# Cleared matrix images in DRAM for the base inverses of a gated DeltaNet, and a last token tile in two column halves

## The chip, the cores and the metric

The kernel runs on one core of a Trainium2 chip. The metric is device time in microseconds (us) of one execution; where several runs are given, it is their median. The engines are named as in the profile: PE is TensorE (PEld its weight loads), DVE is VectorE, ACT is ScalarE, POOL is GpSimd, and SP is SyncE, whose queue issues nearly all DMA transfers of this kernel. L549 means line 549 of the kernel's file.

## The reference

One layer of a bidirectional hybrid encoder: 1024 tokens of width 1024, all in float32. Three sub-layers follow one another, each with an RMS norm before and after it and a residual sum:

- a mixer that is half windowed attention and half a bidirectional gated DeltaNet (4 heads, key and value width 128, chunks of 64 tokens, two directions), with one projection in and one out
- cross attention into 256 memory tokens
- a SwiGLU network of width 2816

The part that the change touches most is the triangular solve of the DeltaNet. For each head, direction and chunk:

```python
tmat = lower + jnp.eye(c, dtype=jnp.float32)
rhs = jnp.concatenate([v * beta[..., None], kb * jnp.exp(g)[..., None]], axis=-1)
sol = lax.linalg.triangular_solve(tmat, rhs, left_side=True, lower=True, unit_diagonal=True)
```

The other part is the end of the layer, `x = x + _rms_norm(f, g_ffn_post)`, where `f` is the product with `w_down`. The norm of a token needs the sum of squares over all 1024 columns of `f`.

## The kernel before, in words

Every product in full precision is made of three matmuls on float32r parts (`split`, L99 to L106: ACT makes the high part, L103, and DVE or POOL the low part, L104). A tile scheduler fixes the order of instructions on each engine when the program is built, from a list of steps written by hand (`ORDER_1`, `ORDER_2`, `ORDER_3`, L37 to L39) and from priorities. Within an engine the order then stands. SP's queue is in order too: a transfer whose wait is not over holds back all that stand behind it, and in the program's own list a transfer also waits for the transfer eight places before it to have landed.

**ORDER_1** (about 20 to 220 us of the profiled execution). Projections of q, k and v with a short convolution (`conv`, L287 on DVE), the decays (E), the turned keys (K), key products (U), query products (C), and `base_inverse` (B, L522 to L556) for each of two groups `g` of two heads. It takes the 32x32 diagonal blocks of the strictly triangular key products, 128 of them side by side (64 in each direction), one per partition, and inverts them by 30 elimination steps on DVE (L545, L547). Two scaled results remain: `V`, the transposed inverses, and `A`, the plain ones, both as 128 partitions of 32x32. Four DMAs (L554) put them into the DRAM tensors `d_inv`, 4 KB a partition.

**ORDER_2** (about 220 to 360 us). Projections for the attention (A, V), the gate (G), the first attention windows (W) and four `levels` (L, L558 to L632), one per head, which build the 128x128 inverses of both directions from the 32x32 ones in two steps (32 to 64, 64 to 128):

- `fetch` (L564) reads four block columns from `d_inv` (`cz` and `cw`, each for two directions, 128 partitions of 8 x 32 numbers, in pieces of 128 bytes). POOL copies strips of them into `m5`, `c5` and `c6` (L575 to L578).
- Each of two parts (4 chunks each) widens `c5`, `c6`, `cz0` and `cz1` into 128x128 matrices with zeros off the diagonal blocks: `D5`, `D6`, `Z0` and `Z1`, by a product with the mask `dmask` on DVE (L588, 128x512 numbers an instruction).
- The part loads `Ul` (key products, L591), transposes it on PE (L595), masks it into `L5` and `L6` on DVE (L596, L597), and makes two pairs of products (L604 and L610): `L5` with `m5`, then `D5` with the result, which fills the second diagonal into `D6`, `Z` and `mov6` (L615 to L624); then `L6` with `mov6`, and `D6` with the result, which fills the last quarter of `Z` (L626, L627). L629 stores both `Z` into `d_pz`.

`D5`, `D6`, `Z0`, `Z1` have two buffers each, so a level's `Z` tiles wait for the stores of the level before. PE takes up matmuls of the projections (L262) between the steps of a level, in the fixed order.

**ORDER_3** (about 360 to 560 us). The scan over chunks, which loads `kv` and `pz` from DRAM, beside the other windows and the memory's keys and values. Then follow the output projection, cross attention and SwiGLU.

**The end.** The last product (L1773 to L1786) takes four token tiles `t`, each of 33 matmuls of 512 columns into one PSUM bank `X[t]`. Behind each tile (L1787 to L1797): add to `zv` (L1791, DVE), sum of squares (`sq_of`, L1706, ACT), gain (L1793, DVE), root by `rstd_at` (L1721 and L1722, POOL), two sums with the residual (L1796, DVE) for the halves `za` and `zv`, and two output writes (L1797). For the last tile nothing is left that this could lie beside.

## Time and profile before

| what | value |
|---|---|
| median of 3 runs | 1525.34 us (1525.03 to 1528.78) |
| the profiled execution, its own time | 1531.03 us |
| its span in the trace | 1529.3 us, 1.7 us less |
| granted PE clock, mean | 0.994 of full |
| DMA moved | 261.06 MB in 275159 packets |

The profile is one execution of 1531.03 us. Stretches and durations are read from it; a difference that is worked out in it is then set against the median. The stage of the levels is found in it by L588 (first at 220.0, last at 340.0 us) and by the stores of L629 (256.3 to 361.7 us). The views used below are: the page; a table of stages (busy time of each engine in a stretch); groups of instructions by line; waits (who waited for whom); the timeline (single instructions); the DMA view; and the chain of work that ended last.

### The profile page before, as it was taken

How to read it: one execution, taken by the hardware profiler on the slowest of the kernel's cores; microseconds unless marked ns; L12 is line 12 of the kernel's file. 1: busy time of each engine (PE TensorE's matmuls, PEld its weight loads, DVE VectorE, ACT ScalarE, POOL GpSimd, SP SyncE). 2: the span in 40 equal slices, each digit the busy share in tenths (PEclk: the TensorE clock that was granted, in tenths of full speed). 3: DMA queues.
4: the chain of work that ended last, by engine and by line, in shares of the span. 5: the costliest groups of instructions: out<-in, count | busy, mean ns of one | idle time of the engine just before them, and what ended most of it. 6: DMA issues, size and time to landing. Idle time of an engine off the chain costs nothing.

```text
span 1529.3 us, 21202 instructions
## 1 busy us (share of the span) xinstructions
PE 1475.7 (96%) x7403; PEld 1239.1 (81%) x7403; DVE 1116.3 (73%) x1805; ACT 752.0 (49%) x1541; POOL 364.1 (24%) x369
## 2 busy tenths in 40 slices
PE   6999999998999999999999999999999999999997
PEld 5888888877889778888788877888888888888786
DVE  6868999787888866538567768676867774696665
ACT  5578821447557764455544685223222332454532
POOL 2020221311226203252201002433534342000021
PEclk9999999999999999999999999999999999999999
DMA  6235575856987584458725554343434333853355
GB/s 208 76 109 148 144 194 142 218 176 173 322 279 236 186 296 152 141 167 271 241 97 173 192 182 134 97 138 116 146 109 153 124 103 111 321 208 97 104 177 167
DMA packets 275159, 261.06 MB, mean 171 GB/s; under 512 B 34904, under 2 KB 206829, under 8 KB 275053
## 3 DMA queue, kind: packets, MB, share of 16 engines
q1 hardware_dynamic: 275053, 259.71, 53.9%
q8 instruction: 58, 0.95, 0.3%
q14 instruction: 48, 0.39, 0.1%
HBM read 181.25 MB, written 75.79 MB: 168 GB/s over the span
## 4 chain that ended last, share of the span: by engine, by line
PE 61%; DVE 10%; DMA 10%; ACT 4%; issue 3%; SPq 2%; POOL 1%; DVEq 0%; POOLq 0%; ACTq 0%
PE pD L1481 7%; PE pE L1481 7%; PE pA L1481 6%; PE pmg L1071 6%; PE pdX L1687 6%; PE pst L1287 5%; PE pcq L262 4%; PE pB L1481 3%; PE psc L810 2%; PE pdA L1687 2%; PE pdD L1687 2%; PE pg L262 2%; DMA wraw<-in_w_gate_up_dram 1%; PE pco L1186 1%; PE pdX L1784 1%
## 5 line engine op out<-in xcount | busy, mean ns | idle before, releaser
L103 ACT CAST whi<-wraw 128x1024 fp32r<-128x1024 f32 x96 | 100.8, 1051 | 133.0 <-DMA wraw<-in_w_gate_up_dram 37.0
L262 PE MATMUL pg<-hlo,whi 128*128 128x512 f32 x352 | 139.1, 396 | 0.0
L262 PE MATMUL pg<-hhi,whi 128*128 128x512 f32 x352 | 139.1, 396 | 0.0
L262 PE MATMUL pg<-hhi,wlo 128*128 128x512 f32 x352 | 138.1, 393 | 0.0
L104 POOL TENSOR_TENSOR wlo<-wraw,whi 128x1024 fp32r<-128x1024 f32 x36 | 88.3, 2453 | 189.6 <-ACT whi L103 188.2
L1481 PE MATMUL pA<-b,whi 128*128 128x512 f32 x352 | 111.9, 400 | 3.6 <-ACT m L1508 2.8
L104 DVE TENSOR_TENSOR wlo<-wraw,whi 128x1024 fp32r<-128x1024 f32 x60 | 76.0, 1269 | 46.0 <-ACT whi L103 42.4
L1481 PEld LDWEIGHTS pA<-b,whi 128*128 128x128 f32 x352 | 66.5, 192 | 19.2 <-ACT m L1508 4.0
L1687 PE MATMUL pdX<-dhl,whi 128*128 128x512 f32 x264 | 76.1, 390 | 1.5 <-ACT dhl L103 0.8
L262 PEld LDWEIGHTS pg<-hhi,whi 128*128 128x128 f32 x352 | 66.3, 189 | 13.4 <-ACT hhi L103 0.2
L262 PEld LDWEIGHTS pg<-hhi,wlo 128*128 128x128 f32 x352 | 66.2, 188 | 12.8
L262 PEld LDWEIGHTS pg<-hlo,whi 128*128 128x128 f32 x352 | 66.2, 188 | 12.7
L1564 POOL TENSOR_TENSOR act<-act,up 128x512 f32<-128x512 f32 x33 | 50.7, 1538 | 83.1 <-DVE up L1563 61.8
L1481 PE MATMUL pA<-b,wlo 128*128 128x512 f32 x176 | 69.9, 398 | 0.5 <-DVE wlo L104 0.5
L103 ACT CAST whi<-araw 128x1024 fp32r<-128x1024 f32 (+1 forms) x36 | 35.3, 982 | 67.9 <-PE pdX L1687 27.6
L104 DVE TENSOR_TENSOR wlo<-araw,whi 128x1024 fp32r<-128x1024 f32 (+1 forms) x36 | 40.9, 1135 | 36.1 <-ACT whi L103 35.7
L1536 POOL TENSOR_TENSOR sr<-wraw 128x512 f32<-128x512 f32 x22 | 30.3, 1379 | 150.7 <-DMA wraw<-in_w_gate_up_dram 98.7
L287 DVE SCALAR_TENSOR_TENSOR acc<-cp,cols,acc 128x1024 f32<-128x1024 f32 x48 | 62.1, 1297 | 0.1
L1687 PEld LDWEIGHTS pdX<-dhl,whi 128*128 128x128 f32 x264 | 49.3, 188 | 12.7 <-ACT dhl L103 1.1
L1721 POOL TENSOR_SCALAR frs<-sq 128x1 f32<-128x1 f32 x8 | 11.9, 1497 | 194.5 <-ACT jk L1706 193.6
L103 ACT CAST dhl<-b 128x512 fp32r<-128x512 f32 x66 | 40.3, 620 | 31.6 <-PE pdA L1687 13.7
L1481 PE MATMUL pB<-s0h,s1h 128*128 128x512 f32 x176 | 54.5, 391 | 0.0
(484 smaller groups left out, 4285.5 us busy)
## 6 DMA issues: line engine op xcount, KB each, us to landing
wraw<-in_w_gate_up_dram SPq DMA_DIRECT2D x54, 512.0 KB, 3.9
kv<-d_kv SPq DMA_DIRECT2D x32, 512.0 KB, 7.5
wraw<-in_w_in_dram SPq DMA_DIRECT2D x22, 512.0 KB, 4.2
b<-in_w_down_dram SPq DMA_DIRECT2D x20, 512.0 KB, 8.0
araw<-d_as SPq DMA_DIRECT2D x20, 512.0 KB, 3.7
pz<-d_pz SPq DMA_DIRECT2D x32, 256.0 KB, 7.6
wraw<-in_w_ckv_dram SPq DMA_DIRECT2D x16, 512.0 KB, 6.3
wraw<-in_w_out_dram SPq DMA_DIRECT2D x16, 512.0 KB, 3.7
```

Source lines behind the costliest of these rows:

```text
L103: nc.scalar.copy(hi, src)
L104: return (eng or nc.vector).tensor_tensor(lo, src, f32(hi), ALU.subtract)
L262: nc.tensor.matmul(p_, w[:, k, :], ah[a][:, k, :], start=(k == 0 and i == 0), stop=(k == nk - 1 and i == 2))
L287: nc.vector.scalar_tensor_tensor(acc, cp[:, t:t + S], taps[t], acc, ALU.mult, ALU.add)
L810: nc.tensor.matmul(out[:, d, h, :], lt[:, d, h, :], rt[:, d, h, :], start=True, stop=True)
L1071: nc.tensor.matmul(pp[t], act[a][:, k, tt], w_[:, kk, :], start=(k == 0 and i == 0), stop=(k == KT - 1 and i == 2))
L1186: nc.tensor.matmul(po, vr_[a][:, kt, cs], pts[kt][b_], start=(kt == 0 and i == 0), stop=(kt == 1 and i == 2))
L1287: nc.tensor.matmul(bank, a[:, tt], w, start=(start and i == 0), stop=(stop and i == 2), skip_group_check=not check)
L1481: nc.tensor.matmul(out_, w[a][:, k, :], xx[b_][:, k, :], start=(start and k == 0 and i == 0), stop=(k == HK - 1 and i == 2), skip_group_ch ...
L1536: nc.gpsimd.tensor_tensor(s[0], b_[:, 0:HK], b_[:, HK:], ALU.add)
L1564: nc.gpsimd.tensor_tensor(o_, o_, up, ALU.mult)
L1687: nc.tensor.matmul(banks[t], a[:, k - k0, tt], w, start=(first and k == 0 and i == 0), stop=(k == NB - 1 and i == 2), skip_group_check=not ...
```

## The change

1. *Images in DRAM.* `d_inv` goes. For each group a tensor `d_lv` holds 16 sets (2 heads x 8 chunks) of 128 rows; a row of a set is four matrix rows of 128 numbers side by side (`D5`, `D6`, `Z0`, `Z1`), 2 KB. `clear` writes zeros into all of it: eight DMAs of 1 MB from a zero tile of 128x512 numbers, which POOL fills once and which lies where the tile `vt` lies later. `ORDER_1` names them as Z.
2. `base_inverse` writes the 32x32 blocks straight onto the diagonals of these images (`diagonal`), and the rows for `m5` into `d_m5`: ten DMAs for a group instead of four. All but the two for `d_m5` go in pieces of 128 bytes.
3. `levels` loads `m5` (128 KB, pieces of 128 bytes) and, for each part, one tile `DZ` with all four matrices (1 MB, rows of 2 KB; three buffers). `fetch`, the POOL copies, the four DVE widenings of a part and `dmask` go. `z5` and `mov6` have one buffer instead of two.
4. *The end.* The last token tile is made in two halves of 256 columns; the second half accumulates in a bank of its own (`XL`), its share of the old sum being added to `zv` beforehand. For all four tiles of the second half of the tokens, the root is now taken by Sqrt on ACT and a reciprocal on DVE (`inverse_root`, which the kernel already has) instead of POOL's power.

```diff
-ORDER_1 = ("k0 k1 E0 K0 U0 E1 K1 U1 S0 q0 v0 ...
+ORDER_1 = ("k0 k1 Z E0 Z K0 Z U0 Z E1 Z K1 Z U1 Z S0 q0 Z v0 ...
...
-    d_inv = [[dram.tile([2, 2, NT, 4, 32, 32], F32, name=f"d_inv{g}{i}") for i in range(2)] for g in range(2)]
+    LW, LB_ = 4 * P, 32 * 4 * P + 32
+    d_lv = [dram.tile([1, 8 * NT * LB_ + LW], F32, name=f"d_lv{g}") for g in range(2)]
+    d_m5 = [dram.tile([8 * NT, 32, 32], F32, name=f"d_m5{g}") for g in range(2)]
+    def diagonal(g, kind):
+        at = kind * P
+        return (d_lv[g][0, at:at + 8 * NT * LB_].rearrange("(n y) -> n y", y=LB_)[:, 0:32 * LW]
+                .rearrange("n (r w) -> n r w", w=LW)[:, :, 0:32])
+    def level_rows(g, x0):
+        return (d_lv[g][0, 0:8 * NT * LB_].rearrange("(x y) -> x y", y=4 * LB_)[x0:x0 + 4, 0:P * LW]
+                .rearrange("x (p w) -> p x w", w=LW))
...
-    dmask = sm.tile([P, 4, 32], F32, name="dmask")
-    nc.gpsimd.memset(dmask, 0.0)
-    for q in range(4):
-        nc.gpsimd.memset(dmask[32 * q:32 * q + 32, q, :], 1.0)
+    zero = t2.tile([P, 4, P], F32, tag="vt", name="zero").rearrange("p c n -> p (c n)")
+    nc.gpsimd.memset(zero, 0.0)
+    cleared = [0]
+    def clear():
+        g, x0 = cleared[0] // 4, 4 * (cleared[0] % 4)
+        cleared[0] += 1
+        nc.sync.dma_start(level_rows(g, x0), bc(zero, 1, (P, 4, LW)))
...
-        for i in range(2):
-            for d in range(2):
-                nc.sync.dma_start(d_inv[g][i][d].rearrange("h c b r s -> (h c b) r s"),
-                                  (A if i == d else V)[64 * d:64 * d + 64])
+        for d in range(2):
+            first, second = (A, V) if d == 0 else (V, A)
+            lo_, hi_ = 64 * d, 64 * d + 64
+            nc.sync.dma_start(d_m5[g][1 - d::2], second[lo_ + 1 - d:hi_:2])
+            nc.sync.dma_start(diagonal(g, 0)[d::2], first[lo_ + d:hi_:2])
+            nc.sync.dma_start(diagonal(g, 2 + d), second[lo_:hi_])
+            for q in (2 * d, 2 * d + 1):
+                nc.sync.dma_start(diagonal(g, 1)[q::4], first[lo_ + q:hi_:4])
...
-        def fetch(dst, i, d):
-            nc.sync.dma_start(dst, d_inv[g][i][d, hh].rearrange("c b r s -> (b r) c s"))
-        cz = [blocks("cz0"), blocks("cz1")]
-        cw = [blocks("cw0"), blocks("cw1")]
-        m5, c5, c6 = blocks("m5"), blocks("c5"), blocks("c6")
-        for d in range(2):
-            fetch(cz[d], 1, d)
-            fetch(cw[d], 0, d)
-        for q in range(4):
-            r = slice(32 * q, 32 * q + 32)
-            nc.gpsimd.tensor_copy(m5[r], cz[1 - q % 2][r])
-            nc.gpsimd.tensor_copy(c5[r], cw[q % 2][r])
-        for d in range(2):
-            nc.gpsimd.tensor_copy(c6[64 * d:64 * d + 64], cw[d][64 * d:64 * d + 64])
+        m5 = blocks("m5")
+        nc.sync.dma_start(m5, d_m5[g][32 * hh:32 * hh + 32].rearrange("(c b) r s -> (b r) c s", b=4))
...
-            L5, L6, D5, D6 = wide("L5"), wide("L6"), wide("D5"), wide("D6")
-            Z = [wide("Z0"), wide("Z1")]
-            for e, dst, src in ((nc.vector, D5, c5), (nc.vector, D6, c6), (nc.vector, Z[0], cz[0]), (nc.vector, Z[1], cz[1])):
-                e.tensor_tensor(dst.rearrange("p c (q n) -> p c q n", q=4), bc(src[:, c4, :], 2, (P, 4, 4, 32)),
-                                        bc(dmask, 1, (P, 4, 4, 32)), ALU.mult)
+            L5, L6 = wide("L5"), wide("L6")
+            DZ = tl_.tile([P, 4, 4, P], F32, tag="DZ", name="DZ", bufs=3)
+            nc.sync.dma_start(DZ.rearrange("p c k n -> p c (k n)"), level_rows(g, hh * NT + 4 * b))
+            D5, D6, Z = DZ[:, :, 0], DZ[:, :, 1], [DZ[:, :, 2 + d] for d in range(2)]
...
+    nc.vector.tensor_tensor(zv[:, 3, 256:], zv[:, 3, 256:], X[3][:, 256:], ALU.add)
+    XL = bank("pdY")
...
+        columns = [(slice(0, 512), X[t])] if t < 3 else [(slice(0, 256), X[t][:, 0:256]), (slice(256, 512), XL[:, 0:256])]
+        for c_, p_ in columns:
+            fresh = c_.start > 0
+            for k, (ah, al) in enumerate(tiles):
                 for i, (a, w) in enumerate(((ah, t4h), (ah, t4l), (al, t4h))):
-                    nc.tensor.matmul(X[t], a[:, k], w[:, k0 + k], start=False, stop=(k0 + k == NB - 1 and i == 2),
-                                     skip_group_check=True)
+                    nc.tensor.matmul(p_, a, w[:, k, c_], start=(fresh and k == 0 and i == 0), stop=(k == NB - 1 and i == 2),
+                                     skip_group_check=not fresh)
...
-        nc.vector.tensor_tensor(zv[:, t], zv[:, t], X[t], ALU.add)
-        sq_of(zv[:, t], r, 0)
-        nc.vector.tensor_tensor(zv[:, t], zv[:, t], gp[:, 0:512], ALU.mult)
-        rs = rstd_at(r)
+        known = sq[:, 1, r:r + 1]
+        nc.vector.tensor_scalar(known, known, D * EPS, None, ALU.add)
+        for c_, p_ in columns:
+            nc.vector.tensor_tensor(zv[:, t, c_], zv[:, t, c_], p_, ALU.add)
+            sq_of(zv[:, t, c_], r, 0)
+            nc.vector.tensor_tensor(zv[:, t, c_], zv[:, t, c_], gp[:, c_], ALU.mult)
+            if c_.stop < 512:
+                nc.vector.tensor_tensor(known, known, sq[:, 0, r:r + 1], ALU.add)
+        rs = tp_.tile([P, 1], F32, tag="frs", name="frs")
+        inverse_root(rs, sq[:, 0, r:r + 1], 1.0, known)
```

`inverse_root` is this:

```python
def inverse_root(rs, ss, scale, bias):
    nc.scalar.activation(rs, ss, AF.Sqrt, bias=bias, scale=scale)
    nc.vector.reciprocal(rs, rs)
```

21 lines of the change are left out of this document (12 added, 9 removed).

## The prediction

> **What bounds the kernel now.** I read the page first: the span and the busy share of each engine.
>
> ```profile
> span 1529.3 us, 21202 instructions
> PE 1475.7 (96%) x7403; PEld 1239.1 (81%) x7403; DVE 1116.3 (73%) x1805; ACT 752.0 (49%) x1541; POOL 364.1 (24%) x369
> ```
>
> TensorE looks full over the whole span. That is an average, so next comes the table of stages (columns: busy time of each engine with its number of instructions, the granted clock, the DMA share, GB/s).
>
> ```profile
> core 0: us, PE busy (x) PEld busy (x) DVE busy (x) ACT busy (x) POOL busy (x), PEclk, DMA share, GB/s
> 180.00:220.00 40.00, 40.00 (x211) 34.02 (x209) 39.02 (x59) 15.06 (x47) 8.39 (x9) 1.00 0.64 164
> 220.00:360.00 140.00, 134.59 (x755) 114.08 (x754) 111.75 (x245) 55.10 (x128) 31.86 (x52) 1.00 0.65 173
> 360.00:560.00 200.00, 185.54 (x1281) 167.63 (x1280) 163.64 (x403) 130.53 (x326) 63.95 (x76) 0.97 0.83 257
> ```
>
> The levels of the triangular inverse, which the change rebuilds, run from 220 to 360 us. In those 140 us TensorE stands idle 140 - 134.59 = 5.4 us. VectorE is busy 39.02 of 40 us just before and 111.75 of 140 us in the stage. So VectorE is heavily loaded there, yet TensorE hardly waits for it. Whatever VectorE work is saved, the time can shrink only by the holes in TensorE's row. Which holes belong to the levels is told by TensorE's waits from 215 to 362 us (total, times, longest):
>
> ```profile
> PE ps L604 <- DVE mov L622: 1.5, 2, 0.8
> PE ps L604 <- DVE L L597: 0.8, 3, 0.4
> PE ps L595 <- DMA Ul<-d_u: 0.8, 1, 0.8
> PE ps L595 <- DVE Z L627: 0.8, 1, 0.8
> PE ps L595 <- DVE Z L588: 0.5, 1, 0.5
> ```
>
> Eight waits, 4.4 us. A matmul's end is modelled late, so a hole is longer than its row: in the tail, 19 steps lie between the two 512-column matmuls below, that is 0.227 us a step, while each is drawn as 0.39 us.
>
> ```profile
> 1517.20 0.39 PE L1784 MATMUL pdX<-t4l,whi 128*128 128x512 f32 x1
> 1521.51 0.39 PE L1784 MATMUL pdX<-t4h,wlo 128*128 128x512 f32 x1
> ```
>
> Each hole is therefore up to 0.16 us longer: 4.4 + 8 x 0.16 = 5.7 us in the levels' own lines. Seven of the eight, 3.6 + 7 x 0.16 = 4.7 us, end on VectorE; one, 0.8 us, on a DMA. This is the purse of the change's large part.
>
> **The change part by part.** *Expansion and copies that go.* Each level widened four block columns into matrices on VectorE, for which GpSimd first copied strips (groups from 215 to 362 us; busy, mean ns, idle before):
>
> ```profile
> L588 DVE TENSOR_TENSOR Z<-cz,dmask 128x512 f32<-128x512 f32 x16 | 11.3, 724 | 7.3 <-DMA d_pz<-Z 7.0 <-DMA cz<-d_inv 0.3
> L588 DVE TENSOR_TENSOR D<-c,dmask 128x512 f32<-128x512 f32 x16 | 11.2, 713 | 1.0 <-POOL c L576 1.0
> L576 POOL COPY c<-cw 32x256 f32<-32x256 f32 x16 | 8.6, 540 | 13.1 <-DVE D L588 8.9 <-DVE wlo L104 3.4
> L575 POOL COPY m<-cz 32x256 f32<-32x256 f32 x16 | 8.5, 531 | 15.5 <-DMA cz<-d_inv 10.3 <-PE ps L604 4.7
> ```
>
> VectorE loses 16 x 0.724 + 16 x 0.713 = 23.0 us and the 8.3 us of waiting in front of them, GpSimd at least 17 us. Nearly all of that lay beside TensorE's projections. TensorE's order in the changed program is the old one to within a few matmuls (a level's transposes stand 0 to 6 us of matmul time later or earlier), so the gain is the seven VectorE holes, at most 4.7 us. I take 4.2: `mov` and `L` still pass through VectorE, only with less ahead of them. The attention windows of 300 to 360 us share VectorE; I take another 0.5 us for them, from nothing up to 1.5.
>
> *What replaces them.* The images hold 128-byte pieces in DRAM. Per group of two heads the base inverse now issues 10 stores where it issued 4: 2 of m5 rows and 8 diagonals with 2 x (1024 + 2048 + 1024) = 8192 pieces, 1.05 MB. Each level loads m5 and two tiles `DZ` of 1 MB each, in 2 KB rows, where it loaded four 128 KB blocks in 128-byte pieces. Together 8 x 1 MB in, 16 x 128 KB out of the old list. The DMA rows of the stretches from the first inverse to the levels' loads:
>
> ```profile
> 185.00:195.00 10.00, 10.00 (x55) 8.50 (x54) 9.94 (x12) 3.79 (x19) 3.49 (x3) 1.00 0.78 190
> 195.00:215.00 20.00, 20.00 (x106) 17.09 (x105) 19.75 (x30) 7.25 (x22) 4.42 (x3) 1.00 0.56 155
> 215.00:232.00 17.00, 15.67 (x80) 12.75 (x79) 14.59 (x27) 2.27 (x4) 5.83 (x11) 1.00 1.05 235
> ```
>
> The last of them in 40 slices of 0.425 us (GB/s, from the DMA view of that stretch):
>
> ```profile
> GB/s 293 287 305 327 352 283 274 204 205 150 176 181 175 155 135 125 216 298 316 341 334 225 300 327 299 288 302 298 249 256 124 154 86 202 148 185 87 205 306 236
> ```
>
> No row shows a 128-byte store to DRAM. The first four loads of levels 0, in 128-byte pieces, are the dent of slices 8 to 16, 125 to 205 GB/s: at that rate 1.05 MB take 5 to 8 us, my bound from below. From above, a piece costs what two 512-byte pieces cost at the stretch's 235 GB/s: 8192 x 1024 bytes / 235 GB/s = 36 us. I take 8 us, nearer the loads, which have the same size. Between 185 and 215 us the DMA engines have 10 x 0.22 + 20 x 0.44 = 11 us free: 8 us fit, 36 do not. The `DZ` loads cost 1 MB / 235 GB/s = 4.5 us each at the worst rate, 36 us for eight; 0.35 x 140 = 49 us are free in the stage, less what the old 128-byte loads give back. In the burst at 215 us three of them stand in one line with the `Ul` loads, so the hole of 0.8 us on `Ul` stays.
>
> The Trainium skill speaks against this part: its page "DMA: Bandwidth & Descriptors", section Specifications, wants at least 512 bytes for the full rate and says that a smaller transfer is done as read-modify-write. No row here shows it for stores; in 128-byte loads the dent above agrees, a half to two thirds of the rate beside it. By that rule a store would cost more than these loads, up to the bound from above, and the third rival below would be the result.
>
> *Waits that are added.* `DZ` has three buffers, so the last part of levels 3 waits until the stores of the first part of levels 2 have landed, before its first product with `DZ` (before, only the later `Z` tiles waited for a store). In the old run:
>
> ```profile
> 328.58 0.51 SPq L922 DMA_DIRECT2D mt<-in_mem_dram  x1
> 331.07 7.06 DMA d_pz<-Z
> 345.55 0.97 PE L610 MATMUL ps<-bs,D 128*128 128x32 f32 x8
> ```
>
> The new load stands behind `mt` in SP's queue, so it issues near 331, and even with the 7.06 us that a store took to land there it is in by 338 or 339; the product comes at 345.55. Slack about 6 us. Of the 6 us some 2 are left if TensorE comes 4.2 us earlier. The second part of levels 1 waits in the same way for the first stores of levels 0; behind it in SP's queue stand `Ul`, the rotations' copies `rr` and the next projection weights, and behind the last load the level stores and the scan's first `kv` loads. At worst each holds SP for the 7.06 us above. A second weight buffer covers that with the 48 x 0.227 = 10.9 us of matmuls of one projection; the scan needs `kv` only in the stage from 360 us. I charge nothing; without the cover, 3 us each.
>
> *Clearing.* Eight stores of 1 MB zeros stand in SP's order around the second of the two loads of `posi` and ahead of two weight loads (the queue's row is of 32 to 72 us: packets, MB, share; in the others: start, duration, group):
>
> ```profile
> q1 hardware_dynamic: 5488, 2.69, 24.1%
> 34.31 4.84 SPq L384 DMA_DIRECT2D posi<-in_positions_dram  x2
> 46.71 6.77 SPq L125 DMA_DIRECT2D wraw<-in_w_in_dram  x2
> 68.06 1.03 ACT L103 CAST whi<-wraw 128x1024 fp32r<-128x1024 f32 x1
> ```
>
> From 32 to 72 us the queue is 24.1% used, so 30 us are free. 8.4 MB at 235 GB/s, or at the 257 / 0.83 = 310 GB/s of a full share in the scan's stage, take 27 to 36 us: the clears end at 62 to 71 us and the weights land 2 to 4 us behind them, against a cast at 68.06. On the fast side they are hidden; on the slow side the cast waits some 7 us, and the second weight buffer's 10.9 us cover that. The second `posi` lands behind four clears, 14 to 18 us after 35; VectorE takes it up two weight splits and three convolution steps later than it did. I charge nothing; if that cover is gone, up to 7 us. The zero memset and the loss of the mask's memsets fall where GpSimd idles.
>
> *Last tile in halves.* 33 matmuls of 512 columns become 66 of 256. Eleven steps between two 256-column matmuls elsewhere give 0.121 us:
>
> ```profile
> 457.59 0.29 PE L950 MATMUL pck<-mT,whi 128*128 128x256 f32 x1
> 458.92 0.28 PE L950 MATMUL pck<-mT,whi 128*128 128x256 f32 x1
> ```
>
> 66 x 0.121 - 33 x 0.227 = +0.5 us. The end of the old run after the last matmul:
>
> ```profile
> 1521.93 0.69 DVE L1791 TENSOR_TENSOR zv<-zv,pdX 128x512 f32<-128x512 f32 x1 [3.02 <-PE pdX L1784]
> 1522.71 0.63 ACT L1706 ACTIVATE jk<-zv 128x512 f32<-128x512 f32 x1 [6.79 <-DVE zv L1791]
> 1523.25 0.19 ACT L1706 ACTIVATION_READ_ACCUMULATOR jk<-zv 128x1 f32 x1
> 1523.53 0.80 POOL L1721 TENSOR_SCALAR frs<-sq 128x1 f32<-128x1 f32 x1 [6.07 <-ACT jk L1706]
> 1524.41 0.56 POOL L1722 TENSOR_TENSOR frs<-frs,mhalf 128x1 f32<-128x1 f32 x1
> 1525.01 0.75 DVE L1796 SCALAR_TENSOR_TENSOR za<-za,frs,xrf 128x512 f32<-128x512 f32 x1 [0.84 <-POOL frs L1722]
> ```
>
> Add and square of half the width: an estimate of 0.40 and 0.42 for 0.69 and 0.63, between all and half of the rows, -0.5 us (nothing to -0.66). From 1523.44 to 1525.01, 1.57 us, GpSimd took the root; now ScalarE's Sqrt and VectorE's reciprocal, for which the nearest small rows are these:
>
> ```profile
> 64.68 0.26 ACT L335 ACTIVATE za<-za 128x64 f32<-128x64 f32 x1
> 340.75 0.18 DVE L670 RECIPROCAL es<-es 128x4 f32<-128x4 f32 x1
> ```
>
> 0.26 + 0.18 and two hops of 0.06: 0.56, -1.0 us (bounds: -1.2 and, if each took GpSimd's time, 0). One more output piece costs an estimated 0.1, the fixed part of one more VectorE instruction. Sum: +0.5 - 0.5 - 1.0 + 0.1 = -0.9 us. Sqrt needs one table load, 1.28 us by the first row; it falls into the 2.39 us that ScalarE idles ahead of the second, which hide it:
>
> ```profile
> 55.55 1.28 ACT L288 ACT_TABLE_LOAD   x1 [3.06 <-DVE acc L287]
> 1502.78 0.84 ACT L103 CAST whi<-atr 128x768 fp32r<-128x768 f32 x1 [2.39 <-PE pdX L1784]
> ```
>
> **Sum.** -4.2 - 0.5 - 0.9 = -5.6 us on a profiled execution of 1531.03 us (span 1529.3 and 1.7 around it). The median of the runs is 1525.34, so the same difference gives 1519.7.
>
> **The rivals.**
> *A wait for data takes the place of the VectorE wait.* The level's second product waits for `DZ` or `Ul` in the burst at 215 us and behind SP's stalls on stores. For it: a share of 1.05 there, and three loads of 1 MB. Against it: between a level's first transposes and that product TensorE's order has 42 projection matmuls, 42 x 0.227 = 9.5 us, and some small ones. The 4.7 us stay, the tail's 0.9 is kept, SP's stalls cost 0 to 3: 1524.4 to 1527.5.
> *More than the holes.* VectorE at 39.02 of 40 us paces everything it feeds; with 23 us less and GpSimd quieter the levels end early, the scan starts earlier and the windows run ahead, and half of the 14.5 us that TensorE idles from 360 to 560 us is cut too: -5.6 - 7 = 1512.7. Against it: that stage has its own load (VectorE 163.64 of 200, DMA 0.83).
> *The 128-byte stores are slow (slower than before).* Place: right after each inverse, from 186 us and again from about 258. At the upper bound they take 36 us each; 11 us are free the first time, and 25 us of backlog meet the full stretch at 215 us. The first `DZ` then lands some 25 us late against 9.5 us of slack: 15 us of TensorE idle. The second time the stage's share of 0.65 leaves 0.35 x 40 = 14 us free up to the first product of levels 2, 22 us of backlog against more slack: some 3 us. 1525.34 - 0.9 + 18 = 1542. It decides from 11 + 9.5 = 20.5 us of stores on, that is 20.5 x 16 / 8192 = 40 ns of one DMA engine a piece.
> *The clears hold up the weights*, as priced: up to 7 us on top of the forecast, 1520 to 1527.
>
> **How the numbers follow.** Forecast 0.48 (1516 to 1522.5), more than the holes 0.12, data wait 0.24, slow stores 0.10, clears 0.06. A measurement of this kernel can tell about 0.3%, that is 4.6 us, from no change: faster is below 1520.8. Of the forecast some 0.70 lies there: 0.34 + 0.12 = 0.46. Slower (above 1529.9): slow stores, and a little of the data wait, the clears and costs not seen, 0.16. Same: 0.38. The range 1511 to 1531 leaves out the slow stores past 1531 and the far end of the second rival.
>
> **What would show it.** Right: no L588-like group, VectorE 220 to 360 us near 90 of 140, TensorE idle there down to 1 to 2 us, the last matmul to the last output write 1.4 us shorter. Wrong: TensorE waits named after `DZ`, `Ul` or `m5`; a DMA share over 1 reaching past 195 us; a cast near 70 us that waits for `wraw`. A time above 1530 would mean that the diagonals' stores are slow.

## The result, and the profile after

The changed kernel takes 1542.31 us, the median of 4 runs (1541.32 to 1544.38). The kernel before, run on the same chip, takes 1526.79 us (1525.03 to 1528.78). The ratio is 1.0091, with a 95% interval of 1.0070 to 1.0113; by the medians the change is 15.5 us slower, where 5.6 us faster was forecast. The profiled execution of the changed kernel is one of 1541.32 us with a span of 1539.6 us, 10.3 us longer than that of before. The trace of before is of an execution of 1531.03 us, longer than its median, and that of the changed kernel is of the shortest of its four. So the two traces show 10.3 of the 15.5 us; where the other 5 lie they cannot tell.

The page of the changed kernel, first lines, and then its table of stages:

```profile
span 1539.6 us, 21246 instructions
PE 1481.4 (96%) x7436; PEld 1246.1 (81%) x7436; DVE 1088.8 (71%) x1786; ACT 753.6 (49%) x1548; POOL 336.0 (22%) x317
```

```profile
180.00:220.00 40.00, 37.32 (x194) 31.49 (x193) 35.16 (x51) 15.08 (x46) 8.36 (x10) 0.97 0.65 154
220.00:360.00 140.00, 132.64 (x707) 113.68 (x706) 88.22 (x210) 46.28 (x112) 9.57 (x10) 0.95 0.79 221
```

VectorE lost what it was to lose: 88.22 us of 140 in place of 111.75. But TensorE gets through 707 matmuls in the stage of the levels where it got through 755, at a granted clock of 0.95 in place of 1.00. TensorE's waits from 215 to 362 us (total, times, longest) say where:

```profile
PE ps L613 <- ACT bs L615: 3.1, 1, 3.1
PE ptw L690 <- DVE m L666: 2.9, 1, 2.9
PE ps L462 <- ACT acc L301: 2.7, 1, 2.7
PE ps L604 <- DMA Ul<-d_u: 1.3, 1, 1.3
```

Ten short waits of before, 5.4 us together (the eight of the prediction's list and two of the attention windows), have become four, three of them near 3 us. None of the four is one of the seven that ended on the levels' VectorE work. TensorE stands idle 140 - 132.64 = 7.4 us in the stage, where 1 to 2 were forecast. To see what they cost in time I add up, in the trace, the usual distance to the next start for each TensorE instruction, and ask when each kernel has the same amount of this work behind it. The lag is the difference to the profile of before (us; the columns e... are the runs told of below; "end" is at 1500 us of before):

```
before   after    e1     e2     e3     e5     e9    e10    e13    e16    e18
 210      0.6   -0.1    1.1    1.1    0.8    1.3    1.7    2.0   -0.4   -0.2
 220      5.2   -0.1    3.8    1.1    5.4    4.5    1.7    2.0   -0.4   -0.2
 270      3.0   -1.9    5.5    0.9    3.5    3.4   -0.3    2.8    0.3    1.8
 280      9.8   -1.9    9.8    7.3   10.0    9.2    6.4   10.9    8.8    7.8
 310      8.5   -1.9   10.6   10.5   11.6   11.0    5.5    9.8    7.6    6.9
 330     14.0   -1.9   18.4   12.0   10.9   12.2    4.7   10.8    6.8    6.1
 360     11.5   -0.7   16.1   10.3    9.0   10.8    2.2    9.6    4.4    3.7
 560     11.9   -2.8   16.0   11.4    1.5   10.8   -3.1   26.2    7.6    4.0
 end     11.4    0.0   15.4    9.5    1.2   12.3   -0.6   25.3    4.2    0.9
```

All of the 11 us that the traces show arise between 210 and 330 us, in three steps of 4.6, 6.8 and 5.5 us, one at each hole; behind each, 1 to 2.5 us are won back. e1 differs from before only at the very end, so its column shows how far a lag may wander by itself: 2 to 3 us.

**The hole at 217 us** in the timeline of the changed kernel (start, duration, instruction, in brackets idle time before and its releaser):

```profile
201.24 0.51 SPq L551 DMA_DIRECT2D bB<-d_beta  x1
...
202.73 1.97 DVE L554 SCALAR_TENSOR_TENSOR A<-V,bB 64x1024 f32<-64x1024 f32 x1 [4.29 <-DMA bB<-d_beta]
...
215.79 1.06 ACT L301 ACTIVATE acc<-acc 128x1024 f32<-128x1024 f32 x1 [9.25 <-DVE acc L300]
...
216.90 1.16 PE L462 MATMUL ps<-ident,acc 128*128 128x128 f32 x8 [2.68 <-ACT acc L301]
...
218.28 0.63 PE L275 MATMUL pg<-hlo,whi 128*128 128x512 f32 x1
218.71 0.63 PE L275 MATMUL pg<-hhi,wlo 128*128 128x512 f32 x1
```

and the same two instructions in the kernel before:

```profile
191.20 1.48 SPq L533 DMA_DIRECT2D bB<-d_beta  x2
...
196.60 2.07 DVE L536 SCALAR_TENSOR_TENSOR A<-V,bB 64x1024 f32<-64x1024 f32 x1
```

The second inverse begins with a product that needs `bB`. Its load stood behind four stores in SP's queue, and stands behind ten now: it is issued 10 us later, VectorE idles 4.29 us for it, the convolution behind it on VectorE is late, and TensorE waits 2.68 us. The two last rows of the first fence show a second price: behind the hole two 512-column matmuls start 0.43 us apart, not 0.227. The granted clock of the 7 us around the hole, 215 to 222 us, is 0.76. The 2.68 us cost 4.6.

**The hole at 278 us**, first in the changed kernel, then in the kernel before:

```profile
261.68 0.47 SPq L573 DMA_DIRECT2D d_m<-V  x1
...
262.66 0.69 DVE L767 TENSOR_TENSOR rr<-pg,sct 128x512 f32<-128x512 f32 x1
...
270.50 3.30 SPq L638 DMA_DIRECT2D d_pz<-DZ  x4
...
274.76 1.46 SPq L772 DMA_DIRECT2D rr<-rr  x2
276.38 0.47 SPq L597 DMA_DIRECT2D DZ<-d_lv  x1
276.89 1.20 SPq L772 DMA_DIRECT2D rr<-rr  x2
...
277.57 0.60 ACT L793 ACTIVATE gt<-pg 128x512 f32<-128x512 f32 x1 [11.83 <-DMA d_q<-rop]
278.06 0.26 ACT L615 COPY bs<-ps 128x128 f32<-128x128 f32 x1
278.38 1.16 PE L613 MATMUL ps<-m,L 128*128 128x32 f32 x8 [3.12 <-ACT bs L615]
...
282.93 0.69 DVE L773 TENSOR_TENSOR rop<-rop,rr 128x512 f32<-128x512 f32 x1 [11.80 <-DMA rr<-rr]
```

```profile
261.91 1.80 SPq L762 DMA_DIRECT2D rr<-rr  x3
...
272.12 1.13 SPq L554 DMA_DIRECT2D d_inv<-V  x2
```

`rr` is the half of the rotation that four small copies carry to other partitions; `rop` adds it, goes to `d_q`, and comes back as `qr` for a window. Before, these copies were issued by 263.7 us and the second inverse's stores followed at 272. Now the second inverse is done 10 us earlier, its ten stores and a level's four stores are ahead of the copies, and a 1 MB `DZ` load stands between them. VectorE has the product that they carry done by 263.35 us; they are issued from 274.76 us on, 11 us later. VectorE idles 11.80 us for `rr`. ScalarE idles 11.83 us with `gt`, whose buffer is shared with `rop`; the level's `bs` stands behind it, and TensorE waits for that.

**The hole at 324 us** in the changed kernel:

```profile
314.72 0.37 SPq L597 DMA_DIRECT2D DZ<-d_lv  x1
...
316.26 2.49 SPq L772 DMA_DIRECT2D rr<-rr  x4
...
321.68 0.69 DVE L773 TENSOR_TENSOR rop<-rop,rr 128x512 f32<-128x512 f32 x1 [5.81 <-DMA rr<-rr]
...
324.22 0.90 PE L690 MATMUL ptw<-ident,sc 128*128 128x128 f32 x3 [2.89 <-DVE m L666]
```

Here the copy was issued right behind `DZ` and `Ul` and came in 5 us later; the median of such copies in the trace of before is 2.0 us. One row of VectorE's waits, 215 to 362 us, holds both waits (11.8 and 5.8 of 22.2 us): first of the changed kernel, then of the kernel before.

```profile
DVE rop L773 <- DMA rr<-rr: 22.2, 4, 11.8
```

```profile
DVE rop L763 <- DMA rr<-rr: 1.8, 1, 1.8
```

**The end** came as forecast (timeline of the changed kernel; the last matmul, of 256 columns, starts at 1533.13):

```profile
1533.45 0.42 DVE L1811 TENSOR_TENSOR zv<-zv,pdY 128x256 f32<-128x256 f32 x1 [0.78 <-PE pdY L1801]
1533.96 0.42 ACT L1716 ACTIVATE jk<-zv 128x256 f32<-128x256 f32 x1 [1.82 <-DVE zv L1811]
...
1534.50 0.29 ACT L1320 ACTIVATE frs<-sq 128x1 f32<-128x1 f32 x1
1534.85 0.16 DVE L1321 RECIPROCAL frs<-frs 128x1 f32<-128x1 f32 x1
```

From the start of the last matmul to the end of the span it is 1539.60 - 1533.13 = 6.47 us, where it was 7.80. From the first matmul of the last tile it is 14.58 us, where it was 15.67: 1.1 us won.

### The profile page after: what moved, and what is told of

The parts are those of the page before. It is cut to its first block, busy times and chain, and to the rows that moved or that the text cites. A ratio compares the mean times of both kernels' runs of the same rounds, so it can differ in the third digit from the quotient of the medians.

```text
span 1539.6 us, 21246 instructions
## 1 busy us (share of the span) xinstructions
PE 1481.4 (96%) x7436; PEld 1246.1 (81%) x7436; DVE 1088.8 (71%) x1786; ACT 753.6 (49%) x1548; POOL 336.0 (22%) x317
## 4 chain that ended last, share of the span: by engine, by line
PE 77%; DVE 9%; DMA 7%; ACT 3%; issue 2%; SPq 2%; POOL 1%; DVEq 0%; ACTq 0%; POOLq 0%
PE pg L275 10%; PE pE L1491 8%; PE pD L1491 8%; PE pA L1491 6%; PE pmg L1081 6%; PE pdX L1697 6%; PE pst L1297 5%; PE pcq L275 4%; PE pB L1491 4%; PE psc L820 3%; PE pdA L1697 2%; PE pdD L1697 2%; PE pco L1196 1%; PE pdX L1801 1%; DMA b<-in_w_down_dram 1%
## 5 line engine op out<-in xcount | busy, mean ns | idle before, releaser
L1491 PE MATMUL pD<-b,s0h 128*128 128x512 f32 x176 | 54.2, 389 | 0.0
```

The costliest lines, as they stand in the source:

```text
L1491: nc.tensor.matmul(out_, w[a][:, k, :], xx[b_][:, k, :], start=(start and k == 0 and i == 0), stop=(k == HK - 1 and i == 2), skip_group_ch ...
```

## The experiments

Theory Q says that places in SP's queue cost the time, theory L that the `DZ` loads delay the rotations' copies, theory T that the new bytes do so whatever queue they stand in, theory P (the prediction's rival) that 128-byte pieces are slow. Beside each run stands before on the same chip; no time is compared across chips, only ratios.

**e1: the new end alone.**

```diff
 (kernel before)
-        nc.vector.tensor_tensor(zv[:, t], zv[:, t], X[t], ALU.add)
...
+        for c_, p_ in columns:
+            nc.vector.tensor_tensor(zv[:, t, c_], zv[:, t, c_], p_, ALU.add)
```

> Only part 4, the new end, on the kernel before. By the prediction's sum 0.9 us less than before, some 1525.9 against 1526.8; by the trace of after, where the delay of TensorE's last matmuls is 11.4 us and that of the span 10.3, some 1.1 us less. A rival, that the two bank halves and the Sqrt with its table load cost what they save, gives no difference. So small a difference is read from the trace's end, from the last matmul to the last output write: 1.4 us shorter by the prediction.

Measured: 1528.16 us against 1528.49, ratio 0.9993 (0.9974 to 1.0013). The interval cannot show 1 us. The trace can: from the first matmul of the last tile to the end 14.58 us, as in the changed kernel, 1.1 us less than before. Part 4 is a small gain, and parts 1 to 3 cost the whole of the loss.

**e2: the scalars early.**

```diff
+        if g == 0:
+            for k in range(2):
...
+                    nc.sync.dma_start(bt[64 * d:64 * d + 64], bv[d])
+        bB, b1 = betas[g]
```

> The changed kernel, but the first inverse loads the scalars bB and b1 of both groups, ahead of its stores. Theory Q (SP's queue: the ten stores hold what stands behind them): the second inverse no longer waits 4.3 us for bB, TensorE's hole at 217 us and the half-speed matmuls behind it go, some 4.5 us less than after: 1537.8. Theory P (128-byte pieces are slow in DRAM and delay the DZ images): no difference, 1542. Theory L (the 1 MB DZ loads delay the rotations' copies): no difference up to 270 us, so 1542 as well.

Measured: 1544.48 against 1528.49, ratio 1.0095 (1.0058 to 1.0132). Theory Q in the form that I had given it missed: the hole is there (2.4 us at 220 us). VectorE's row in this run names another holder:

```profile
203.92 1.99 DVE L560 SCALAR_TENSOR_TENSOR A<-V,bB 64x1024 f32<-64x1024 f32 x1 [4.84 <-DMA d_lv<-V]
```

`A` has one buffer, and the second inverse may not write it before the first one's stores have landed. The ten stores hold the second inverse in two ways, and one was open.

**e3: four stores of whole 4 KB pieces**, and **e4: ten stores in whole pieces.**

```diff
 (e3)
-        for d in range(2):
-            first, second = (A, V) if d == 0 else (V, A)
...
+        flat = d_lv[g][0, 0:128 * 1024].rearrange("(n r w) -> n r w", r=32, w=32)
+        nc.sync.dma_start(d_m5[g][0:32], V[0:64:2])
+        nc.sync.dma_start(d_m5[g][32:64], A[64:128:2])
+        nc.sync.dma_start(flat[0:64], V[0:64])
+        nc.sync.dma_start(flat[64:128], A[64:128])
 (e4)
-            nc.sync.dma_start(diagonal(g, 0)[d::2], first[lo_ + d:hi_:2])
-            nc.sync.dma_start(diagonal(g, 2 + d), second[lo_:hi_])
+            nc.sync.dma_start(flat[32 * d:32 * d + 32], first[lo_ + d:hi_:2])
+            nc.sync.dma_start(flat[64 + lo_:64 + hi_], second[lo_:hi_])
```

> The changed kernel with four stores of 4 KB pieces per group instead of ten; what the levels read from the images is then not the inverses, so part of the computation is left out, at the same number of instructions elsewhere. Theory Q: the holes at 217 and 278 us shrink or go, 8 to 11 us less than after: 1531 to 1534. Theory L: the holes at 278 and 324 us stay, only the one at 217 goes: 1537 to 1538. Theory P: all three go, and the forecast of the prediction comes true: 1520 to 1526.

> The changed kernel with its ten stores per group of the same partitions, but each in pieces of 4 KB instead of 128 bytes (contents of the images left out as in the run with four stores). It tells the number of stores from the size of their pieces. Theory Q (the number of DMA instructions in SP's queue and their places count): as after, 1540 to 1543. Theory P (the pieces count): as with four stores, 1520 to 1534. Theory L: as after.

Measured: e3 1541.19, ratio 1.0069 (1.0041 to 1.0097); e4 1542.67, ratio 1.0075 (1.0052 to 1.0098). Theory P falls: with ten stores in whole pieces the time is that of 128-byte pieces within the intervals, where P named 1520 to 1534. In e3 the hole at 217 us is gone (lag 1.1 before it and behind it). In e4 it has shrunk to 0.7 us, VectorE waiting 1.90 us for `bB`; whether by the size of the pieces or by the order of SP's queue there, no run tells. But the totals hardly move. In e3 the other two holes stay; e4 has holes of 2.4 us at 230 (`Ul`), 2.2 at 291 and 3.0 at 324. TensorE's waits in e3, 200 to 362 us:

```profile
PE ps L616 <- ACT bs L612: 3.9, 2, 3.3
PE psw L661 <- DVE m L663: 3.3, 1, 3.3
```

**e5: DZ loads issued by ScalarE**, **e6: rotations' copies by ScalarE**, **e7: stores by ScalarE**, **e8: stores and DZ loads by ScalarE.**

```diff
 (e5, e8)
-            nc.sync.dma_start(DZ.rearrange("p c k n -> p c (k n)"), level_rows(g, hh * NT + 4 * b))
+            nc.scalar.dma_start(DZ.rearrange("p c k n -> p c (k n)"), level_rows(g, hh * NT + 4 * b))
 (e6)
-                nc.sync.dma_start(rot[32 * q:32 * q + 32], sn[o:o + 32])
+                nc.scalar.dma_start(rot[32 * q:32 * q + 32], sn[o:o + 32])
 (e7, e8)
-            nc.sync.dma_start(diagonal(g, 0)[d::2], first[lo_ + d:hi_:2])
+            nc.scalar.dma_start(diagonal(g, 0)[d::2], first[lo_ + d:hi_:2])
...
```

> The changed kernel with the eight DZ loads of 1 MB issued by ScalarE, on its own DMA queue, in place of SP's. Theory L (the rotations' copies rr wait in the same queue behind a DZ load): rr lands some 2 us after its issue again, the holes of TensorE at 278 and 324 us go, the one at 217 stays: 9 to 12 us less than after, 1530 to 1533. Rival T (the transfers themselves are too many, whatever the queue): rr still takes 5 us or more, 1540 to 1544. Rival A (ScalarE is held by the loads' waits): slower than after.

> The changed kernel with the rotations' copies rr issued by ScalarE in place of SP. They then stand neither behind the ten stores nor behind DZ. Theory L with Q: the holes at 278 and 324 us go, the one at 217 (bB) stays: 9 to 12 us less than after, 1530 to 1533. Rival T: rr takes 5 us or more all the same, 1538 to 1544. Rival A: ScalarE, in order, waits for VectorE's product ahead of each copy and is late with its own work: no gain, or slower.

> The changed kernel with the ten stores of each inverse issued by ScalarE. Theory Q: the second inverse no longer waits for bB in SP's queue, though its A still waits until the stores of the first A have landed; the hole at 217 goes or halves, and rr is no longer held at 262 to 274 us: 4 to 8 us less than after, 1534 to 1538. By L alone the holes at 278 (in part) and 324 stay. Theory P (128-byte pieces): no difference.

> Both, the ten stores and the eight DZ loads, issued by ScalarE. If Q and L together are the whole cost and do not overlap, 14 to 17 us less than after, 1525 to 1528, and TensorE's lag behind the kernel before stays within 2 us from 220 to 360 us; if the forecast's gain on VectorE's holes then comes through, 1520 to 1524. Rival A: ScalarE's queue takes SP's part, and little is gained: 1536 or more.

Measured, ratios to before at 1530.46 us: e5 1533.30, 1.0029 (1.0014 to 1.0044); e6 1542.56, 1.0089 (1.0056 to 1.0122); e7 1551.43, 1.0137 (1.0117 to 1.0157); e8 1537.94, 1.0050 (1.0033 to 1.0067). e5 has the time that L forecast, but not for L's reason alone. The hole at 324 us is gone, yet the other one has grown to 5.6 us: ScalarE now has the `DZ` loads in its own order and issues the second of two only at 282.97 us; `gt`, at 283.80 after 7.49 us of idle time, and the `bs` for which TensorE waits, at 288.24, come behind it. So rival A had a part in it. Most of e5's better time comes later, between 360 and 560 us (lag 9.0 to 1.5). Two more rows of e5, SP's and VectorE's:

```profile
276.11 0.66 SPq L772 DMA_DIRECT2D rr<-rr  x1
...
282.91 0.69 DVE L773 TENSOR_TENSOR rop<-rop,rr 128x512 f32<-128x512 f32 x1 [9.07 <-DMA rr<-rr]
```

The copy took 6.8 us although `DZ`, issued at 275.56, stood in another queue. So the other queue does not keep it clear of `DZ`; a level's store of 256 KB, issued at 275.53 on SP's own queue, is a second candidate that this row does not rule out. The Trainium skill, page "DMA: Bandwidth & Descriptors", section "Queues, rings and completion order", says that SP's and ScalarE's rings lie on the same sixteen engines; this row agrees with that. In e6 the holes at 278 and 324 us come down to 1.0 and 1.3 us, but three others of 0.9 to 2.0 us are new, and the lag at 290 us is 10. Its time is that of the rivals T and A, which this run does not tell apart. In e7 and e8 ScalarE, in order, is held by the stores: in e7 it idles 19.18 us ahead of the `bs` at 274 us, in e8 15.35 us at 272. Rival A holds in e8, and the same happens in e7, whose expectations were both missed.

**e9: a quarter of each DZ load**, and **e10: that with four stores.**

```diff
...
-            nc.sync.dma_start(DZ.rearrange("p c k n -> p c (k n)"), level_rows(g, hh * NT + 4 * b))
+            nc.sync.dma_start(DZ[:, 0:1].rearrange("p c k n -> p c (k n)"), level_rows(g, hh * NT + 4 * b)[:, 0:1])
...
```

> The changed kernel with a quarter of each DZ load: one of the four chunks, 256 KB in place of 1 MB, into three tiles that GpSimd clears once ahead of the levels; the other chunks then have no inverses, so part of the computation is left out, at the same instructions on TensorE, VectorE and ScalarE. Theory T (the bytes of the images: they fill the DMA engines in bursts, and the rotations' copies and the other loads land late, whichever queue issues them): the holes of TensorE at 278 and 324 us go, the one at 217 (second inverse behind the ten stores) stays: 9 to 12 us less than after, 1530 to 1534 where before is 1527 to 1530. Rival S (not the bytes but the places in SP's queue and its rule of eight transfers under way): no difference, the same holes. Rival P (the 128-byte stores): no difference.

> The quarter of each DZ load and four stores of whole 4 KB pieces together (both leave the inverses out, as in the runs with one of them). If the stores (hole at 217 us) and the bytes of DZ (holes at 278 and 324 us) are the whole cost, the forecast's gain is what remains: 4 to 6 us less than before, 1521 to 1525 where before is 1527 to 1529. If VectorE's holes were not the purse that the prediction took them for, the same as before.

Measured, before 1528.67: e9 1541.61, ratio 1.0089 (1.0071 to 1.0107); e10 1530.16, ratio 1.0009 (0.9994 to 1.0025). The bytes make the hole at 324 us: in e9 TensorE waits 0.8 us there (`ptw` for `m`), in place of 2.9, and the copy issued at 314.55 us lands in 2.5 us, where 5.4 were needed in the changed kernel. But they do not make the one at 278 us. It stays in e9 (2.3 us) and also in e10, 3.7 us with neither ten stores nor large loads; theory T as the whole cause falls, and the total of e9 is the one that rival S named. e10 has a lag of 0 before it, 6.4 behind it and -0.6 at the end. It reaches only the time of before, not the forecast's 4 to 6 us less.

**e11: the price of a hole by its length.**

```diff
...
+            for k in range(64):
+                nc.tensor.matmul(ps, a, w, start=(k == 0), stop=(k == 63))
+            nc.vector.tensor_scalar(c, ps[:, 0:P], 0.001, None, ALU.mult)
+            for _ in range(n):
+                nc.vector.tensor_scalar(c, c, 0.5, None, ALU.mult)
...
```

> Not the kernel: blocks of 64 matmuls of 128x512, between which TensorE waits for a chain of VectorE instructions of growing length, twelve lengths three times over; the output is not the reference's. It shows the price of a hole in TensorE's row by its length. By the traces so far: after holes under 1.5 us the next matmuls start 0.227 us apart, after holes of 2.7 to 3.3 us they start 0.427 us apart for some 4 us, which costs 2 us more. Rival: the slow matmuls in those traces come from the neighbours of the hole (DMA bursts, weight loads) and not from the idle time; then they do not appear here at any length up to 5 us.

Measured, TensorE's timeline, two blocks of 64 matmuls (idle time as drawn; by starts the holes are 0.16 us longer):

```profile
86.64 14.79 PE L101 MATMUL ps<-w,a 128*128 128x512 f32 x64 [2.31 <-DVE a L107]
```

```profile
353.63 17.35 PE L101 MATMUL ps<-w,a 128*128 128x512 f32 x64 [3.35 <-DVE a L107]
```

By starts: after holes of 0.8 to 1.95 us none of 12 blocks has slow matmuls; after 2.47 and after 2.99 us two of three each; from 3.5 to 7.2 us all 17. A slow block has 7 to 12 starts 0.427 us apart and costs 1.5 to 2.7 us, no more after 7 us than after 3.5. The granted clock is 1.00 over the first block above and 0.84 over the second. The idle time alone does it, and the rival falls. The Trainium skill, page "TensorE: Matmul & The Clock Gate", section "HAM oscillation — how this bites in real kernels", warns of holes over some 3.4 us. Here 2.5 us can be enough, so the measurement decides. That equal holes do and do not trigger it agrees with the free-running window of which the Trainium skill speaks on the same page, section "What's actually happening".

**e12: a buffer of its own for gt**, **e13: an own A and early scalars**, **e14: e12 and e5**, **e15: all three.**

```diff
 (e12, e14, e15)
-            gt = trp.tile([P, HALF], F32, tag="rop", name="gt")
+            gt = trp.tile([P, HALF], F32, tag="gt", name="gt", bufs=1)
...
 (e13, e15; with e2's edit)
-        A = tb.tile([P, 32, 32], F32, tag="A", name="A", bufs=1)
+        A = (tb1 if g else tb).tile([P, 32, 32], F32, tag="A", name="A", bufs=1)
...
```

> The changed kernel with a buffer of its own for the gate's gt, which shared two with the rotated rop (z5 lies in L5 to make room). Theory G (ScalarE, in order, waits with gt for the store of rop and holds the level's bs behind it): the hole at 278 us goes, 5 to 7 us less than after, 1535 to 1537 where before is 1527 to 1529. Rival: the next in line, the window's qs that waits for qr, holds bs in gt's place; then a hole of 2 us or more stays there and the time with it, 1540 to 1543.

> The changed kernel with the scalars bB and b1 of both groups loaded ahead of the first stores, and an A of its own for the second inverse, which so waits neither for its scalars in SP's queue nor for the landing of the ten stores. By theory Q the hole at 217 us goes: 4 to 5 us less than after, 1537 to 1538. If the hole stays, the stores hold the convolution in another way.

> Own buffer for gt and the DZ loads issued by ScalarE. The holes at 278 and 324 us go, the one at 217 stays: 11 to 13 us less than after if the three are the whole cost, 1529 to 1531; if each cure moves the cost elsewhere, 1533 or more, as with DZ on ScalarE alone.

> All three: own A and early scalars, own buffer for gt, DZ loads issued by ScalarE. If the three holes are the whole of the cost, the forecast's gain remains: 1521 to 1526, faster than before by 2 to 6 us. If the new transfers cost time wherever they stand, 1529 to 1536.

Measured, before 1530.64: e12 1544.65, ratio 1.0096 (1.0069 to 1.0123); e13 1555.50, 1.0171 (1.0143 to 1.0199); e14 1533.06, 1.0014 (0.9999 to 1.0028); e15 1570.10, 1.0258 (1.0234 to 1.0282). Theory G missed, and so did its rival, which had named `qs`: ScalarE waits for the next entry of SP's late queue instead, the store of the gate before. The run gave `gt` one buffer of its own where it had shared two, so it does not tell what a `gt` without any such wait would do.

```profile
284.83 0.60 ACT L793 ACTIVATE gt<-pg 128x512 f32<-128x512 f32 x1 [13.11 <-DMA d_gate<-gt]
```

e13 shows the hole at 217 us gone with all ten stores in place (lag 2.0 and 2.0, then down to -1.3 at 250 us). With e2 and e3 that settles this hole: the stores hold the second inverse by the scalars and by `A`. But at 270 us `Ul` is 3.0 us late, and the lag grows by 16 us more from 360 to 560 us. e14 is not clear of before, and e15 missed both of its expectations by 30 us or more. Each cure gives the planner another order; why these orders cost what they do after 360 us was not followed up.

**e16: no widening, nothing new transferred.**

```diff
 (kernel before)
-            L5, L6, D5, D6 = wide("L5"), wide("L6"), wide("D5"), wide("D6")
...
-                e.tensor_tensor(dst.rearrange("p c (q n) -> p c q n", q=4), bc(src[:, c4, :], 2, (P, 4, 4, 32)),
-                                        bc(dmask, 1, (P, 4, 4, 32)), ALU.mult)
+            L5, L6 = wide("L5"), wide("L6")
+            D5, D6, *Z = sets[set_at[0] % 2]
...
```

> The kernel before without its 32 widening products on VectorE (L588): the four matrices of a part lie in two sets of tiles that GpSimd clears once, and no inverse is put in, so part of the computation is left out; stores, loads and GpSimd's copies stay as before. It is the gain side of the forecast alone. If VectorE's holes were the purse: 4 to 5 us less than before, 1522 to 1525 where before is 1527 to 1529. If the freed VectorE itself does the damage (the plan pulls steps forward into SP's queue): slower than before by some us, 1530 to 1540. If nothing waits for it: the same.

Measured: 1536.72 against 1528.65, ratio 1.0045 (1.0023 to 1.0067). This run takes the forecast's main term by itself. VectorE is freed (88.20 of 140 us, as in the changed kernel), the DMA traffic is that of before (173 GB/s in the stage in both), and the kernel is 7 us slower by the ratio, 8 by the medians, with a hole at 280 us:

```profile
255.69 1.12 SPq L554 DMA_DIRECT2D d_inv<-V  x2
...
261.64 2.89 SPq L764 DMA_DIRECT2D rr<-rr  x4
264.57 0.58 SPq L565 DMA_DIRECT2D cz<-d_inv  x1
...
270.10 0.53 SPq L766 DMA_DIRECT2D d_q<-rop  x1
...
272.81 0.60 ACT L785 ACTIVATE gt<-pg 128x512 f32<-128x512 f32 x1 [7.57 <-DMA d_q<-rop]
276.60 0.62 ACT L644 CAST qs<-qr 128x512 fp32r<-128x512 f32 x1 [3.18 <-DMA qr<-d_q]
...
280.28 3.64 PE L602 MATMUL ps<-mov,L 128*128 128x64 f32 x16 [5.27 <-DVE mov L620]
```

The second inverse's stores are issued at 255.69 us instead of 272.12, ahead of the rotations' copies instead of behind them, and the next level's loads of `d_inv` follow from 264.57 us instead of 275.92, ahead of the rotated half's store to `d_q` at 270.10. `gt` waits for that store, `qs` for the load of what it stored, and the level's copies stand behind `gt` and `qs` on ScalarE. VectorE's waits for `rr` are 15.1 us in this run, against 1.8. Its plan is not the changed kernel's, though: added up as for the lag, the levels' transposes and products stand up to 11.6 us of matmul time earlier in TensorE's order than before, and in the changed kernel within 3 us of their old places (one transpose 5.5 us). So e16 shows what a freed VectorE can do, not its share of the 15.5 us.

**e17: the changed kernel with VectorE filled up again.**

```diff
+            for _ in range(4):
+                nc.vector.tensor_tensor(L5.rearrange("p c (q n) -> p c q n", q=4), bc(m5[:, c4, :], 2, (P, 4, 4, 32)), ...
```

> The changed kernel with four products of 128x512 on VectorE added to each part of a level, with m5 as their source and L5 as their place, where the widenings were: all new stores and loads, and VectorE as busy as before. If the plan with a free VectorE is the cause, the holes at 278 and 324 us go and the time comes back to 1527 to 1533. If the stores and the bytes are the cause wherever they stand, 1542 or more.

Measured: 1548.16 against 1528.65, ratio 1.0122 (1.0101 to 1.0144). At one place the old order does come back. VectorE is busy 100.23 of the 140 us, and the second inverse's stores stand behind the rotations' copies again (timeline of SP):

```profile
259.65 5.90 SPq L775 DMA_DIRECT2D rr<-rr  x7
...
277.87 0.48 SPq L573 DMA_DIRECT2D d_m<-V  x1
```

The hole at 278 us is gone with it: TensorE has no wait of 0.7 us or more between 272 and 303 us, and the lag falls from 6.7 at 270 to 5.7 at 290 us. But the time does not come back, so the new stores and loads cost time beside a busy VectorE too: holes of 2.3 us at 217, 2.5 at 231 (`Ul`), 4.3 at 304 (a late `qr` load) and 3.9 at 382 us. The padding also brings a wait of its own, since it reads `m5`: VectorE idles 7.43 us for that load at 296 us.

**e18: the first gate ahead of the rotations, in e16.**

```diff
-ORDER_2 = "L0 L1 A4 V A0 A1 G0 G1 L2 L3 W W W A2 A3 G2 G3 W".split()
+ORDER_2 = "L0 L1 A4 V G0 A0 A1 G1 L2 L3 W W W A2 A3 G2 G3 W".split()
```

> The run without widenings (inverses left out as there), with the first gate G0 moved ahead of the rotations A0 and A1 in ORDER_2. ScalarE's order then has the level's bs and z5 ahead of gt and qs. If that order is what opens the hole at 280 us, the hole goes and the lag of 8.5 us with it: 1522 to 1528 where before is 1527 to 1530. If the hole has another cause (SP's queue, the rotations' copies on VectorE), it stays, or moves: 1533 or more.

Measured: 1536.20 against 1529.17, ratio 1.0051 (1.0030 to 1.0072); the profiled execution is the shortest of its six, 1531.71. ScalarE's order is cured: `z` runs at 270.34 us without a wait for a DMA. The wait is now on VectorE, where the level's transposes stand behind `rop`:

```profile
274.60 0.69 DVE L765 TENSOR_TENSOR rop<-rop,rr 128x512 f32<-128x512 f32 x1 [7.26 <-DMA rr<-rr]
```

Two holes of 2.1 and 0.8 us remain in place of 5.3, and the lag still rises by 6 at 280 us. So ScalarE's order alone is not the root. Both engines, in order, wait for the same late copies.

## Why the prediction was wrong, step by step

- **VectorE's work that goes**: right. The L588 group is gone, VectorE is at 88.22 of 140 us where 90 was named.
- **"TensorE's order in the changed program is the old one to within a few matmuls ..., so the gain is the seven VectorE holes"**: the conclusion is the step that failed, -4.2 us in the sum. TensorE's own order held (see e16), and the seven holes went. But the sum let everything else start when it had started before, and the freed VectorE changed the order between the engines and SP's queue. With it the second inverse ends 10 us earlier, its transfers come ahead of the rotations' copies, and a hole opens at 278 us that costs 6.8 us of lag. e16, with a freed VectorE and nothing new to transfer, has such a hole and loses 7 us; in e17, with VectorE filled up and all the new transfers, it is gone. Whether the gain itself was there is not shown: in e13 and e15 the lag falls by 3.3 us from 220 to 250 us, but in e1, with the widenings, by 1.4, and in e16 not at all.
- **"At worst each holds SP ... A second weight buffer covers that ... I charge nothing"**: failed too, a term put at nothing. I had named `rr` among the transfers behind `DZ` and then gave the weights' cover for all of them. VectorE's `rop` has no cover: 22.2 us of waits, the hole at 324 us, 5.5 us of lag (gone in e5 and e14, 0.8 us in e9). TensorE's wait there is one of an attention window, so the 0.5 us that the sum credits to the windows turned into a part of this.
- **The ten stores**: I compared their bytes with the DMA engines' free time, 8 us in 11, and that held. SP's queue was not counted: 6 stores more put `bB` 10 us back, and `A` waits for the landing. The hole at 217 us, 4.6 us, is gone in e3 with four stores, and in e13 with ten of them but an inverse that waits for none.
- **Each hole's own price** was taken as its length. Near 3 us it costs 4.6 to 6.8 us in this kernel; e11 shows 1.5 to 2.7 us of it as matmuls at 0.427 in place of 0.227 us. The rest of the dearest one, at 278 us, some 1 us, is not traced.
- **The slow stores, 1542**: the right time by a mechanism that did not occur. No wait of an engine is named after the loads of `DZ` or `m5` (TensorE's one after `Ul` grew from 0.8 to 1.3 us, which is all that came of the data-wait rival), and in e4 the size of the pieces changes no total that can be measured. The DMA view of the changed kernel from 186 to 202 us gives the packets' price:

```profile
DMA packets 11809, 2.77 MB, mean 173 GB/s; under 512 B 9038, under 2 KB 11745, under 8 KB 11809
q1 hardware_dynamic: 11809, 2.77, 84.9%
```

  0.849 x 16 us x 16 engines / 11809 = 18 ns a packet, all sizes together, under the 40 ns from which that rival was to decide. The Trainium skill, page "DMA: Bandwidth & Descriptors", section Specifications, asks for at least 512 bytes for the full rate. The traces agree as to the engines: they are 84.9% busy here for 2.77 MB, and 71.3% for 3.00 MB in the same stretch of e4. In the kernel's time that makes no difference that can be measured.
- **Clears**: right. The lag at 80 us is -0.1.
- **The end**: right, -1.1 us where -0.9 was forecast.

What stays open: which single entry of SP's queue makes the copies late at 262 to 278 us. e3, e10, e16 and e18 each took other entries away, and the hole moved between ScalarE and VectorE but stayed. That a freed VectorE is enough to open it is shown by e16, and e17 closes it; that a different order would give the forecast's gain was not shown by any run. Nor do the holes add up to the times: each run has a plan of its own, e10 keeps one hole and ends at the time of before, and e15 has its three cures and is the slowest. e10, e14 and e1 are within their intervals of before, and no version beat it.

## What to carry to other kernels

Before a busy engine is relieved, list what its relief lets start earlier, and look where that stands in the queues that are served in order: here SP's queue, whose late entries hold ScalarE and VectorE, mattered more than any engine's busy time. Count a new DMA by its place in its queue and by who waits behind it, not by its bytes against free bandwidth, and give each waiter its own cover. Count a hole of 2.5 us or more in TensorE's row as its length plus some 2 us or more (1.9 to 3.7 here).

## What the runs showed of the hardware that I had not expected

- TensorE's clock drops after an idle time of as little as 2.5 us, in some cases and not in others, for 7 to 12 matmuls of 512 columns at 0.427 us (granted clock 0.84 over such a block of 64, 1.00 over one without); after holes of up to 1.95 us never in 12 cases (e11).
- A small copy issued 0.5 to 1.5 us behind a 1 MB load lands 5 to 7 us after its issue, on the same queue or with the load on the other one (e5: 6.8 us, there with a store of 256 KB ahead of it on its own queue). About 2 us is usual, but it takes no `DZ`: behind loads of `cz`, `cw`, `Ul` and weights, two copies in the trace of before took 5.8 and 4.7 us at 224 us. Behind a quarter of the load it was 2.3 to 2.6 us (e9).
- In a stretch where 9038 of 11809 packets are under 512 bytes, most of them rows of 128 bytes stored to DRAM, a packet costs 18 ns of one DMA engine on average. Whole pieces of 4 KB in their place do not change the kernel's time by what can be measured (e4).
